# Three 64-row score products for two heads at once, q and k split whole, and a new order of the mixer

## The chip, the core and the metric

The kernel runs on one core of a Trainium2 chip. The metric is the device time of one execution in microseconds, the median of the runs. The engines are TensorE (PE in the profile, its weight loads PEld), VectorE (DVE), ScalarE (ACT), GpSimd (POOL) and SyncE (SP), which issues most transfers.

## The reference, cut to what matters

One layer of an encoder over 512 positions of width 1024: a half-step gated feed-forward, a mixer, a second half-step feed-forward, and a final norm. The mixer's attention part is what the change touches most:

```python
h = rms_norm(x, mix_norm)
u = h @ w_in                      # fourier group (512) | q (8x64) | k (2x64) | v (2x64)
q = rms_norm(q.reshape(b, s, N_Q_HEADS, HEAD_DIM), q_norm)
k = rms_norm(k.reshape(b, s, N_KV_HEADS, HEAD_DIM), k_norm)
q, k = apply_axial_rope(q, tables), apply_axial_rope(k, tables)
...
scores = jnp.einsum('bqhgd,bkhd->bhgqk', q_blk, k).astype(jnp.float32) * scale
p = jax.nn.softmax(scores, axis=-1).astype(v.dtype)
return jnp.einsum('bhgqk,bkhd->bqhgd', p, v)
```

Everything is float32. Eight query heads of 64 channels share two key heads (heads 0 to 3 the first, 4 to 7 the second). The mixer's other half is a two-dimensional Fourier transform with a small linear map for each of four channel groups, and both halves go through one output projection.

## The kernel before

**Two-part products.** TensorE multiplies in a rounded form of float32 (`F32R`). To keep float32's accuracy each operand is split into a high part (a rounded copy, made by ACT with `nc.scalar.copy`) and a low part (what is left, made by DVE in `lows`), and a product is made as three: high by high, high by low, low by high (`product`). Most of the kernel is such products over 128 rows of contraction and 512 positions.

**Stages.** `ffn` runs the first feed-forward: an opening of four gate and up chunks (`opening1`), then chunks made with fewer products (`seven`), and `down`. Its channel sums of squares are turned into a row that scales the outcome: `norm.column` or `sums` sums them on PE, `power` takes the root on POOL, and `row` turns the result on PE (L263) and copies it on ACT. Before the change `opening1` calls `row()` inside the last of its eight steps, after four of that step's twelve products. `tail` (chunk `2 * NF`, the half chunk that is left of 2752 channels) follows the opening.

**The mixer** is written as named steps (`op("name")`), each a few instructions of one engine, and the string `ORDER` names all of them in the order in which every engine's instructions are put in its queue. The engines run their queues in order. Names used below: `k.0` to `k.7`, `q0.0` ... are the eight steps (three products each) of a projection; `wk.r`, `wk.h`, `wk.l` load, round and subtract its weights; `n1.c` turns the running sums of squares `acc` on PE, and DVE then reduces them; `k.sq` squares k, `k.pq` turns the squares on PE, `k.s0` reduces them on DVE, `k.s1` takes the root on POOL, `kw` spreads it on DVE, `kp` turns it on PE and `km` multiplies k by it; `s` is a score step, `m` its maximum on DVE, `e` the exponential on ACT, `g` the reciprocal of the sum, `n` the scaling on ACT, `t` the turn of the probabilities on PE, `h` and `l` their split, `v` the product with the values.

**Scores.** A tile of q holds two heads, one of each key head, in rows 0 to 63 and 64 to 127. Before the change each head has a tile of its own, `qa` or `qb`, with the high part of its 64 channels in one half of the rows and the low part in the other, and the keys lie twice in `kst`, as high over low and as low over high. So two products over all 128 rows give the sum of all four part products of one head, one query block and all 512 keys:

```python
nc.tensor.matmul(turned(sps[n]), q, turned(kst[b][0]), start=True, stop=False)
nc.tensor.matmul(turned(sps[n]), q, turned(kst[b][1]), start=False, stop=True)
```

There are 4 tiles of q, 2 heads and 4 query blocks, so 32 score steps of two products (L1207, L1208).

**Banks.** The eight PSUM banks are handed out by `bank_for` and come back when `read` has been called for each reader.

Of the kernel before, what the change touches and what calls it, by code (L numbers as in the profile page):

```python
# [10 lines left out]
ALU = mybir.AluOpType  # L11
# [38 lines left out]
wk.r wq2.r wq0.r wq1.r wk.h wk.l wv.r k.0 k.1 wq0.h k.2 wq0.l k.3 wq1.h k.4 k.5 k.6 k.7 n1.c k.sq q0.0 cos  # L50
wq2.h q0.1 k.pq q0.2 q0.3 n1.m k.rc f0.r q0.4 q0.5 k.s0 q0.6 wq2.l k.s1 q0.7 k.sw q0.sq q2.0 wq1.l kw kp wv.h
q0.pq q1.0 k.rs q0.rc q2.1 q1.1 q1.2 q0.s0 q1.3 km q1.4 q0.sw k0.0 wv.l k1.0 q1.5 q1.6 q0.rs q0.ah q0.bh k0.3
q1.7 k0.2 k1.1 q1.sq k1.3 k0.1 q2.2 wq3.r q2.3 q1.sw q0.al q0.s1 k1.2 v.0 q0.bl q2.4 s001 s002 q1.rc s011
wq3.h m001 s010 m011 pos q2.5 s013 v.1 q1.sd q2.6 m010 e011 q2.7 e001 m002 m013 wq3.l s012 e002 s000 e010
e013 v.2 m012 f1.r q2.sq q2.sw v.3 q1.rs f0.h q3.0 v.4 e012 s003 g01 g02 v.5 f3.r m003 q1.ah q1.pq q3.1 v.6
q2.sd m000 q3.2 n002 v.7 q1.bh n001 q1.s0 n012 q1.al e000 e003 q1.s1 q1.bl f1.h s103 n1.p q3.3 g00 q3.4 g03
q2.rc vt n000 q3.5 n003 vp m103 t000 f1.l vs t003 n011 f0.l n010 q3.6 e103 n013 q3.7 t001 h000 h001 t002
q2.rs q3.sw s101 l001 v.h f00.0 l000 f2.r h002 m101 s110 q2.bh s111 l002 v.l f02.0 m111 q2.bl q3.sq f2.h o0.r
f00.1 s100 e101 f00.u m110 m100 e111 t011 g11 q3.sd s112 v000 v001 m112 h003 q2.pq h011 f02.1 l003 l011 v002
s113 s102 q2.ah q2.s0 n101 q2.s1 e100 e110 v003 t010 n111 f02.e h010 m113 t012 q2.al m102 h012 e113 e102  # L60
q3.rc o00.c t013 g13 f03.0 e112 l010 f02.h g10 f2.l f03.1 f01.0 fw.r o1.r n103 n100 v010 s213 l012 q3.pq g12
h013 o00.a q3.rs n102 f01.1 m213 f3.h f01.u q3.s0 v011 s203 v012 l013 t100 e213 fw.h m203 n110 t101 h100 h101
t102 f3.l t103 v013 l100 f10.0 o01.c q3.ah f10.1 f03.e s210 l101 h102 o01.a f03.h e203 s202 n112 l102 g23
q3.bh s212 v100 m210 n113 n203 v101 m212 h103 e210 fw.l q3.s1 m202 f12.0 t113 f02.l f12.1 r0.h l103 f10.u
q3.al s201 t110 v102 s200 v103 o4.r e212 h113 r0.l f12.e f03.l t111 t112 n213 e202 m200 f11.0 h110 o10.c l110
o10.a f13.0 m201 o2.r h111 e200 f12.h e201 g20 s211 q3.bl o0.h g22 o3.r l111 n200 m211 s303 f11.1 e211 m303
f13.1 n202 map1 f11.u v110 o1.h o5.r l113 map0 o0.l h112 f13.e f12.l d00 s313 map0.h v111 g21 l112 e303
map0.l n201 m313 map1.h s301 d01 f13.h d0.h t200 n210 d10 m301 f13.l d11 h200 n212 d1.h v112 t201 d0.l v113
map1.l c0.s l200 h201 o6.r d1.l t203 o11.c l201 t202 c0.c c0.q c1.s o11.a h203 e313 e301 h202 s312 v200 l203
c0.o c1.c m312 v201 n211 l202 s310 s311 c1.q e312 t210 g33 c0.h t213 h210 o2.h d20 d21 d2.h v202 t211 c1.o  # L70
v203 m310 e310 l210 t212 h211 c1.h d30 m311 h212 o2.l s300 n303 d2.l l211 e311 v210 l212 d31 c2.c c0.l h213
v211 m300 l213 d3.h n313 s302 m302 g31 c2.s v212 e300 c1.l v213 y0.0 y2.0 e302 g30 c2.q o21.c d3.l g32 n311
y2.1 n310 n312 c3.s o1.l c2.o c2.h n302 n300 y0.1 y1.0 c3.c o21.a t311 c3.q o7.r o20.c n301 y1.1 t310 c2.l
y0.2 y2.2 h310 y1.2 c3.o t300 c3.h o20.a t302 t301 l310 h300 c3.l l300 h302 v310 y0.3 r1.h l302 h301 h311
l301 v300 y2.3 t312 l311 v301 t303 v311 h303 t313 h312 r1.l l303 l312 v302 h313 y0.4 v303 y0.5 v312 l313 v313
r2.h y1.3 o30.c y1.4 o31.c y2.4 o30.a o31.a r2.l y1.5 y0.6 r3.h r3.l y0.7 y2.5 o5.h y0.x y0.q y1.6 y1.7 y2.6
o5.l y2.7 y1.x y2.x y5.0 o3.h y5.1 o3.l o6.h y5.2 y2.q o6.l y5.3 y5.4 y3.0 y1.h y3.1 y5.5 y3.2 y2.h y1.l y3.3
y1.q y6.0 y5.6 y5.7 y6.1 y3.4 o4.h o4.l y5.x y3.5 y6.2 y3.6 y3.7 y1.a y0.h y4.0 y0.l y3.x y4.1 y6.3 y3.h y5.h
y4.2 y4.3 y2.l y6.4 o7.h y4.4 o7.l y6.5 y4.5 y4.6 y2.a y4.7 y6.6 y7.0 y3.q y6.7 y7.1 y7.2 y3.a y5.q y7.3 y4.x
y4.q y7.4 y3.l y4.a y5.a y5.l y6.x y7.5 y6.q y6.a y7.6 y6.h y7.7 y6.l y4.h y7.x y4.l y7.q y7.a y7.h y7.l  # L80
# [8 lines left out]
def encoder(ctx, tc, A, out):  # L89
# [89 lines left out]
    def turned(ap):  # L179
        return ap.rearrange("p (a b c) -> p b a c", b=4, c=4)  # L180
# [103 lines left out]
    def ffn(norm, after, wgu, wd, wdt, groups, opening, closing):  # L284
# [6 lines left out]
        with tc.tile_pool(name=f"act{n_}", bufs=1) as ap, tc.tile_pool(name=f"sums{n_}", bufs=2) as sp:  # L291
# [288 lines left out]
            for gi, group in enumerate(groups):  # L580
# [4 lines left out]
                else:  # L585
# [6 lines left out]
                    pss["t"] = [gate(2 * NF)]  # L592
# [128 lines left out]
    def opening1(gate, column, row):  # L721
# [39 lines left out]
        def products(k):  # L761
            hi, lo = ws[k // 2]
            passes = [(c, w, m) for w, m in ((hi, hh), (hi, hl), (lo, hh)) for c in range(4)]
            for n, (c, w, m) in enumerate(passes):
                if (k, n) == (6, 8):
                    sums()
                if (k, n) == (7, 4):
                    row()
                nc.tensor.matmul(
                    turned(pss[c]), w[:, k % 2, c], turned(m[k]), start=False, stop=k == KD - 1 and w is lo,  # L770
                    skip_group_check=True,
                )
# [39 lines left out]
    with tc.tile_pool(name="mix", bufs=1) as mp, tc.tile_pool(name="mixt", bufs=1) as mt:  # L812

        room(mp, 96)
        kst = [[mp.tile([P, S], F32R, name=f"ks{v}{o}") for o in range(2)] for v in range(2)]
# [153 lines left out]
        def query_ops(t):  # L969
# [3 lines left out]
            @op(f"{name}.ah")  # L973
# [627 lines left out]
```

## Time and profile before

| what | value |
|---|---|
| median of 3 runs | 818.72 us |
| lowest run | 818.27 us |
| profiled execution | 818.38 us |
| its span, first to last instruction | 816.6 us |
| PE busy | 809.8 us, 99% |
| DVE busy | 652.4 us, 80% |
| ACT busy | 503.2 us, 62% |
| granted TensorE clock, mean | 0.998 |

A profile row names the line, the engine, the operation, and what it writes and reads; then the count, and the busy time with the mean duration of one in ns, or, in the order of time, the start and the length in us. What stands in brackets is how long the engine had been idle before it and what ended that. "mix" is any of the mixer's banks, "ring" the ring of weight slots, "near" the tiles of q, of the values and of the Fourier half, "ks" the keys.

### The profile page before, as it was taken

The numbers are of one execution on the slowest core, as the hardware profiler recorded it, in microseconds if no ns is written. First come the engines' busy times: TensorE is split into PE (matmuls) and PEld (weight loads), VectorE is DVE, ScalarE is ACT, GpSimd is POOL, SyncE is SP. The second block draws the span as 40 slices with busy tenths as digits, with TensorE's granted clock in tenths as the row PEclk, the third lists the DMA queues.
The fourth block names the chain that finished last, engine by engine and source line by source line (L and its number), as shares of the span: only waits on it lengthen the run. The fifth ranks groups of instructions, "written<-read, shape, count | busy, mean of one in ns | idle before, by whom it ended". The sixth has DMA issues, their size and how long they took to land.

```text
span 816.6 us, 13031 instructions
## 1 busy us (share of the span) xinstructions
PE 809.8 (99%) x4943; PEld 729.3 (89%) x4943; DVE 652.4 (80%) x1083; ACT 503.2 (62%) x871; POOL 67.7 (8%) x75
## 2 busy tenths in 40 slices
PE   9999999999999999999999999999999999999997
PEld 7888998899989998889998888889988998899987
DVE  7997997489856857799998578999955997489674
ACT  7873774267624735699998449557733674267462
POOL 0320000000000000221000003100100000000001
PEclk9999999999999999999999999999999999999999
DMA  7874553345443423442201236554543553345222
GB/s 258 198 172 172 146 132 89 125 130 168 85 151 89 126 67 117 130 149 65 65 26 53 78 109 140 128 188 143 133 116 110 154 145 81 132 130 143 62 78 103
DMA packets 37823, 99.75 MB, mean 122 GB/s; under 512 B 4481, under 2 KB 11265, under 8 KB 37761
## 3 DMA queue, kind: packets, MB, share of 16 engines
q1 hardware_dynamic: 28064, 82.87, 31.2%
q0 software_dynamic: 8832, 15.34, 11.1%
q8 instruction: 38, 0.62, 0.3%
q10 hardware_dynamic: 864, 0.72, 0.3%
q14 instruction: 25, 0.20, 0.1%
HBM read 93.41 MB, written 2.10 MB: 117 GB/s over the span
## 4 chain that ended last, share of the span: by engine, by line
PE 94%; DMA 2%; ACT 1%; DVE 1%; issue 1%; POOL 0%; SPq 0%; POOLq 0%; DVEq 0%; ACTq 0%
PE dn L186 26%; PE r L436 11%; PE mix L186 8%; PE gu L186 8%; PE r L441 8%; PE q L436 4%; PE r L432 4%; PE q L441 4%; PE p L432 4%; PE q L432 4%; PE p L441 2%; PE mix L1267 2%; PE mix L1233 2%; PE mix L1071 1%; PE mix L1072 1%; PE mix L1073 1%
## 5 line engine op out<-in xcount | busy, mean ns | idle before, releaser
L186 PE MATMUL dn<-at,ring 128*128 128x512 f32 x900 | 202.7, 380 | 0.0
L186 PEld LDWEIGHTS dn<-at,ring 128*128 128x128 f32 x900 | 168.0, 188 | 28.9 <-DVE ring L130 0.3
L441 PE MATMUL r<-rt,ring 128*128 128x256 f32 x560 | 154.3, 276 | 0.0
L436 PE MATMUL r<-rt,ring 128*128 128x256 f32 x840 | 147.0, 276 | 0.0
L436 PEld LDWEIGHTS r<-rt,ring 128*128 128x128 f32 x840 | 127.0, 188 | 1.6
L441 PEld LDWEIGHTS r<-rt,ring 128*128 128x128 f32 x560 | 105.1, 188 | 0.2
L391 ACT CAST ring<-s 128x1024 fp32r<-128x1024 f32 x70 | 73.6, 1051 | 35.4 <-PE r L436 16.4
L130 DVE TENSOR_TENSOR ring<-s,ring 128x1024 fp32r<-128x1024 f32 x70 | 85.1, 1216 | 12.6 <-ACT ring L391 10.3
L575 DVE SCALAR_TENSOR_TENSOR gx<-dn,gx 128x512 f32<-128x512 f32 x61 | 41.8, 688 | 63.0 <-PE dn L186 63.0
L172 ACT CAST ring<-raw_dn 128x768 fp32r<-128x768 f32 (+3 forms) x58 | 45.3, 784 | 71.3 <-PE dn L186 55.2
L441 PE MATMUL q<-rt,ring 128*128 128x256 f32 x280 | 77.0, 275 | 0.0
L160 POOL DMA_DIRECT2D ring<-in_wgu x38 | 32.9, 866 | 470.1 <-ACT u L450 372.0
L130 DVE TENSOR_TENSOR ring<-raw_dn,ring 128x768 fp32r<-128x768 f32 (+3 forms) x58 | 51.5, 890 | 9.9 <-ACT ring L172 5.9
L441 PEld LDWEIGHTS q<-rt,ring 128*128 128x128 f32 x280 | 52.6, 188 | 0.0
L130 DVE TENSOR_TENSOR ring<-raw_g,ring 128x1024 fp32r<-128x1024 f32 x35 | 42.6, 1218 | 10.1 <-PE p L432 9.5
L436 PE MATMUL q<-rt,ring 128*128 128x256 f32 x280 | 49.8, 277 | 0.0
L432 PE MATMUL r<-rt,ring 128*128 128x512 f32 x140 | 48.7, 384 | 0.2 <-ACT u L489 0.2
L186 PE MATMUL gu<-ring 128*128 128x512 f32 x216 | 48.9, 381 | 0.0
L432 PE MATMUL q<-rt,ring 128*128 128x512 f32 x140 | 48.3, 382 | 0.0
L432 PE MATMUL p<-rt,ring 128*128 128x512 f32 x140 | 48.3, 382 | 0.0
L186 PEld LDWEIGHTS gu<-ring 128*128 128x128 f32 x216 | 40.4, 188 | 6.9
L391 ACT CAST ring<-raw_g 128x1024 fp32r<-128x1024 f32 x35 | 36.8, 1051 | 15.0 <-DMA raw_g<-in_wgu 12.0
(282 smaller groups left out, 1659.3 us busy)
## 6 DMA issues: line engine op xcount, KB each, us to landing
raw_g<-in_wgu SPq DMA_DIRECT2D x35, 512.0 KB, 3.7
raw_u<-in_wgu SPq DMA_DIRECT2D x35, 512.0 KB, 4.4
raw_dn<-in_wd SPq DMA_DIRECT2D x40, 384.0 KB, 3.2
ring<-in_wgu POOLq DMA_DIRECT2D x35, 256.0 KB, 4.3
raw_gu<-in_wgu SPq DMA_DIRECT2D x12, 512.0 KB, 3.6
raw_o<-in_wo SPq DMA_DIRECT2D x8, 512.0 KB, 3.5
raw_dn<-in_wd SPq DMA_DIRECT2D x8, 448.0 KB, 3.4
raw_wq<-in_wins SPq DMA_DIRECT2D x4, 512.0 KB, 3.6
```

What stands on the lines that cost most here:

```text
L130: nc.vector.tensor_tensor(out=lo, in0=src, in1=asf(hi), op=ALU.subtract)
L160: nc.gpsimd.dma_start(out=lo, in_=src, accum_op=ALU.add)
L172: nc.scalar.copy(hi[:, :n, :], raw[:, :n, :])
L186: nc.tensor.matmul(ps, a, b, start=first and b is mhi and a is whi, stop=last and a is wlo)
L391: nc.scalar.copy(hi, src)
L432: nc.tensor.matmul(turned(ps), whi[:, ks], turned(m), start=start, stop=False, skip_group_check=True)
L436: nc.tensor.matmul(ps[:, t], whi[:, ks], m[:, o * HALF :][:, t], start=start and o == 0, stop=False, skip_group_check=True,)
L441: nc.tensor.matmul(o, wlo[:, ks], m, start=False, stop=stop, skip_group_check=True)
L575: nc.vector.scalar_tensor_tensor(out=x[d][:, t], in0=ps[:, t], scalar=0.5, in1=x[d][:, t], op0=ALU.mult, op1=ALU.add)
L1071: nc.tensor.matmul(ps, hh[k][:, cs], whi[:, a, :], start=k == 0, stop=False)
L1233: nc.tensor.transpose(pts[n][:, c * P : (c + 1) * P], prob[t, b, c][:, kc * P : (kc + 1) * P], ident)
L1267: nc.tensor.matmul(turned(outs[t, b]), w, turned(p), start=kc == 0 and i == 0, stop=kc == 3 and i == 1)
```

## The change

Four things are changed.

1. A score step works on both heads of a tile of q. `qa` now holds the high part and `qb` the low part of the whole tile, `kst[0]` and `kst[1]` those of the keys. For each of the three part products there is one product over rows 0 to 63 (first head) and one over rows 64 to 127 (second head), into two banks; the two alternate. 16 steps of six products take the place of 32 steps of two.
2. Rounding and subtracting q and k is one instruction each over 128 rows, in place of four over 64 rows for each tile of q and eight for k.
3. The maxima of both heads go to one tile of two columns, with one small product for both.
4. The row of the first norm is turned in the tail's chunk, after the first of its eight steps, and no longer in the opening; and `ORDER` is a new one.

```diff
@@ ffn, first group
-                    pss["t"] = [gate(2 * NF)]
+                    pss["t"] = [gate(2 * NF, {} if row else {1: lambda: row.append(norm.row())})]
@@ opening1, products
-                if (k, n) == (7, 4):
-                    row()
@@ query_ops and key_ops
-            @op(f"{name}.ah")
-                nc.scalar.copy(qa[t][0:HD], rots[name][0:HD])
-            @op(f"{name}.al")
-                lows(qa[t][HD:P], rots[name][0:HD], qa[t][0:HD])
-            @op(f"{name}.bh")
-                nc.scalar.copy(qb[t][HD:P], rots[name][HD:P])
-            @op(f"{name}.bl")
-                lows(qb[t][0:HD], rots[name][HD:P], qb[t][HD:P])
+            @op(f"{name}.h")
+                nc.scalar.copy(qa[t], rots[name])
+            @op(f"{name}.l")
+                lows(qb[t], rots[name], qa[t])
...
+            op("k.h")(lambda: nc.scalar.copy(kst[0], rots["k"]))
+            op("k.l")(lambda: lows(kst[1], rots["k"], kst[0]))
@@ score_ops
-                q = (qa, qb)[b][t][:, c * P : (c + 1) * P]
-                sps[n] = bank_for(f"s{n}")
-                nc.tensor.matmul(turned(sps[n]), q, turned(kst[b][0]), start=True, stop=False)
-                nc.tensor.matmul(turned(sps[n]), q, turned(kst[b][1]), start=False, stop=True)
+                sps[n] = [bank_for(f"s{t}{b}{c}") for b in range(2)]
+                cs = slice(c * P, (c + 1) * P)
+                for i, (w, m) in enumerate(((qa[t], kst[0]), (qa[t], kst[1]), (qb[t], kst[0]))):
+                    for b in range(2):
+                        r = slice(b * HD, (b + 1) * HD)
+                        nc.tensor.matmul(
+                            turned(sps[n][b]), w[r, cs], turned(m[r]), start=i == 0, stop=i == 2,
+                            skip_group_check=True,
+                        )
...
-                mxs[n] = mx = tp.tile([P, 1], F32, tag="mx", bufs=8, name=f"mx{n}")
-                nc.vector.tensor_reduce(out=mx, in_=sps[n], axis=AX.X, op=ALU.max, negate=True)
+                mxs[n] = mx = tp.tile([P, 2], F32, tag="mx", bufs=8, name=f"mx{n}")
+                for b in range(2):
+                    nc.vector.tensor_reduce(out=mx[:, b : b + 1], in_=sps[n][b], axis=AX.X, op=ALU.max, negate=True)
                 nc.vector.tensor_tensor(out=mx, in0=mx, in1=f, op=ALU.mult)
@@ ORDER, the start
-wk.r wq2.r wq0.r wq1.r wk.h wk.l wv.r k.0 k.1 wq0.h k.2 wq0.l k.3 wq1.h k.4 k.5 k.6 k.7 n1.c k.sq q0.0 cos
+wq1.r wq0.r wk.r wk.h wk.l wq0.h k.0 cos f1.r k.1 k.2 k.3 k.4 k.5 n1.c wq1.h k.6 wq1.l wq0.l k.7 q0.0 wq2.r q0.1 k.sq
```

What the order of the instructions becomes at three places follows. Lines of the changed program are some numbers lower (L1207 and L1208 are L1190 there, `product` is L182, `lows` L126).

On PE, the first score steps. Before, one head at a time (`ks00` and `ks01` are the two key tiles of the first head, `ks10` and `ks11` of the second):

```order
L186 MATMUL mix4_3304<-ring_61 128x4x32x4 x3
L1207 MATMUL mix3_3303<-ks00_3287,near_3293 128x4x32x4
L1208 MATMUL mix3_3303<-ks01_3288,near_3293 128x4x32x4
L1207 MATMUL mix0_3300<-ks00_3287,near_3293 128x4x32x4
L1208 MATMUL mix0_3300<-ks01_3288,near_3293 128x4x32x4
L1207 MATMUL mix6_3306<-ks10_3289,near_3293 128x4x32x4
L1208 MATMUL mix6_3306<-ks11_3290,near_3293 128x4x32x4
```

Now (`ks0` holds the high, `ks1` the low parts of both heads):

```order
L182 MATMUL mix4_3302<-ring_61,more_3293 128x4x32x4 x6
L1190 MATMUL mix1_3299<-ks0_3287,near_3291 128x4x32x4
L1190 MATMUL mix0_3298<-ks0_3287,near_3291 128x4x32x4
L1190 MATMUL mix1_3299<-ks1_3288,near_3291 128x4x32x4
L1190 MATMUL mix0_3298<-ks1_3288,near_3291 128x4x32x4
L1190 MATMUL mix1_3299<-ks0_3287,near_3291 128x4x32x4
L1190 MATMUL mix0_3298<-ks0_3287,near_3291 128x4x32x4
```

The two heads now alternate between two banks, and a step has six products. Steps that follow each other make blocks: in the whole mixer the 96 products stand in eight blocks, 18, 6 and six times 12.

On DVE, where the first feed-forward ends and the mixer begins (`gx` holds x; `ring` and `more` hold weights and the norm's output; `acc1` the sums of squares). Before:

```order
L575 SCALAR_TENSOR_TENSOR gx_69<-dn0_7_3_3244,gx_69 128x512
L130 TENSOR_TENSOR ring_61<-raw_wq0_3315,ring_61 128x1024
L216 SCALAR_TENSOR_TENSOR ring_61<-gx_69,ring_61 128x512
L228 TENSOR_TENSOR acc1_103<-acc1_103,sq1_7_0_3270 128x512
L1354 TENSOR_REDUCE ms1_105<-mix1_3301 128x4
```

Now:

```order
L571 SCALAR_TENSOR_TENSOR gx_69<-dn0_7_3_3244,gx_69 128x512
L126 TENSOR_TENSOR more_3293<-raw_wq1_3309,more_3293 128x1024
L126 TENSOR_TENSOR ring_61<-raw_wq0_3311,ring_61 128x1024
L212 SCALAR_TENSOR_TENSOR ring_61<-gx_69,ring_61 128x512
L224 TENSOR_TENSOR acc1_103<-acc1_103,sq1_7_0_3270 128x512
L1344 TENSOR_REDUCE ms1_105<-mix1_3299 128x4
```

The subtraction of `wq1` now stands ahead of the norm's last step and of the last addition into `acc1`. On ACT the cast of `wq1` moves in the same way, to just behind that of `wq0` and ahead of the norm's last step.

On PE at the same place, the projections of k (`mix0`) and q0 (`mix2`) and the turns of `acc1` (`n1.c`), of the squares of k (`k.pq`) and of `kw` (`kp`). Before:

```order
L186 MATMUL dn0_7_3_3244<-at0_129,ring_61 128x4x32x4 x18
L186 MATMUL mix0_3300<-ring_61 128x4x32x4 x24
L1350 MATMUL mix1_3301<-ident_107,acc1_103 128x128 x4
L186 MATMUL mix2_3302<-ring_61 128x4x32x4 x6
L954 MATMUL mix3_3303<-ident_107,sq_k_3354 128x128 x4
L186 MATMUL mix2_3302<-ring_61 128x4x32x4 x18
L186 MATMUL mix4_3304<-ring_61 128x4x32x4 x3
L1007 MATMUL mix5_3305<-ident_107,kw_3308 128x128 x4
```

Now:

```order
L182 MATMUL dn0_7_3_3244<-at0_129,ring_61 128x4x32x4 x18
L182 MATMUL mix0_3298<-ring_61 128x4x32x4 x18
L1340 MATMUL mix1_3299<-ident_107,acc1_103 128x128 x4
L182 MATMUL mix0_3298<-ring_61 128x4x32x4 x6
L182 MATMUL mix2_3300<-ring_61 128x4x32x4 x12
L948 MATMUL mix3_3301<-ident_107,sq_k_3361 128x128 x4
L182 MATMUL mix2_3300<-ring_61 128x4x32x4 x9
L182 MATMUL mix4_3302<-ring_61,more_3293 128x4x32x4 x3
L182 MATMUL mix5_3303<-ring_61 128x4x32x4 x3
L182 MATMUL mix2_3300<-ring_61 128x4x32x4 x3
L993 MATMUL mix6_3304<-ident_107,kw_3306 128x128 x4
```

`n1.c` stands six products of k earlier, `k.pq` two steps of q0 later, and `kp` follows it after 18 products in place of 21.

More of the change, by code (lines that the diff above doesn't have):

```diff
@@ L49 @@
 ORDER = """
-wk.r wq2.r wq0.r wq1.r wk.h wk.l wv.r k.0 k.1 wq0.h k.2 wq0.l k.3 wq1.h k.4 k.5 k.6 k.7 n1.c k.sq q0.0 cos
[L51 to L54, printed above, removed]
@@ L1217, in _ @@
[L1217 to L1224 removed]
+            for b in range(2):
+                @op(f"e{t}{b}{c}")
+                def _(b=b):
+                    if t not in zs:
+                        zs[t] = tp.tile([P, 4, 2], F32, tag="z", bufs=2, name=f"z{t}")
+                    prob[t, b, c] = temp(f"e{t}{b}{c}")
+                    nc.scalar.activation(
+                        prob[t, b, c], sps[n][b], AF.Exp, bias=mxs[n][:, b : b + 1], scale=f[:, b : b + 1],
+                        accum_out=zs[t][:, c, b : b + 1],
+                    )
+                    read(f"s{t}{b}{c}")
@@ L1331, in encoder @@
             position_ops(t)
+            for c in range(4):
+                score_ops(t, c)
             for b in range(2):
```

80 lines of the change are left out of this document (30 added, 50 removed).

## The prediction

> **What bounds the kernel now.** I read the page first (busy shares, clock, chain), then busy time by stage, then the order of time at four places.
>
> ```profile
> PE 809.8 (99%) x4943; PEld 729.3 (89%) x4943; DVE 652.4 (80%) x1083; ACT 503.2 (62%) x871; POOL 67.7 (8%) x75
> PEclk9999999999999999999999999999999999999999
> PE 94%; DMA 2%; ACT 1%; DVE 1%; issue 1%; POOL 0%; SPq 0%; POOLq 0%; DVEq 0%; ACTq 0%
> ...
> 330.10:352.00 21.90, 21.90 (x108) 18.50 (x107) 18.14 (x28) 16.77 (x25) 5.79 (x5) 1.00 0.55 180
> 352.00:434.00 82.00, 81.95 (x544) 74.39 (x543) 78.50 (x166) 78.06 (x156) 6.94 (x4) 1.00 0.21 65
> ```
>
> TensorE (PE) is the bound: 99% busy, at full clock, and 94% of the chain that ended last. The two stage rows (length, then busy time of PE, PEld, DVE, ACT, POOL) are the start of the mixer and the attention stage. DVE and ACT are 95% busy in the second, yet PE idles 0.05 us in 82.00. So work taken from DVE and ACT gains nothing; a PE product more or less, or a new PE wait, moves the end by its full size. A product over 512 columns is listed with 0.38 us but the next one starts earlier, so I price products by their starts:
>
> ```profile
> 352.23 0.38 PE L1208 MATMUL mix<-ks,near 128*128 128x512 f32 x1
> 352.45 0.39 PE L1207 MATMUL mix<-ks,near 128*128 128x512 f32 x1
> 352.67 0.38 PE L1208 MATMUL mix<-ks,near 128*128 128x512 f32 x1
> ...
> 371.58 0.28 PE L1072 MATMUL mix<-ring 128*128 128x256 f32 x1
> 371.70 0.28 PE L1073 MATMUL mix<-ring 128*128 128x256 f32 x1
> 371.81 0.28 PE L1071 MATMUL mix<-ring 128*128 128x256 f32 x1
> ...
> L1207 PE MATMUL mix<-ks,near 128*128 128x512 f32 x32 | 12.6, 394 | 0.1
> L1208 PE MATMUL mix<-ks,near 128*128 128x512 f32 x32 | 12.3, 384 | 0.0
> L1208 PEld LDWEIGHTS mix<-ks,near 128*128 128x128 f32 x32 | 6.0, 188 | 0.8
> ```
>
> A score product costs 0.22 us of PE (352.23, 352.45, 352.67). A product over 256 columns costs about 0.115 us although each loads its own weights, so a weight load needs no more than that when it runs beside other work. There are 32 + 32 score products: 64 x 0.22 = 14.1 us.
>
> **The base** is the profiled execution, 818.38 us with a span of 816.6; the median of the runs, 818.72, is 0.04% above it.
>
> **Term 1, the score products.** 64 products over 128 rows become 96 over 64 rows, in 48 pairs: one product of a pair uses rows 0 to 63 and the other rows 64 to 127, they share neither rows nor a bank, and they stand next to each other. No row of the trace has a product over 64 rows, so I bound it. If both of a pair run side by side, the nearest rows are the 512-column product (0.22 us) and two weight loads at the pace of the 256-column rows (2 x 0.115 = 0.23): 48 x 0.23 = 11.0. If they run one after the other, 96 x 0.22 = 21.1. I take the first, since nothing that one product holds is needed by the other: -3.0 us, with -3.5 (0.22 a pair) and +7.0 as ends. The Trainium skill (TensorEngine Tiling (Array Packing), Key Properties) states that different tiles can load and multiply in parallel; no run here shows it yet.
>
> **Term 2, changing between 128 and 64 rows.** The 16 score steps stand in 8 blocks, so there are 16 changes. One may cost nothing, or the tail of a product that the next one otherwise covers: 0.38 - 0.22 = 0.16 us. I take the middle, 0.08: +1.3 us (0 to 2.6). The Trainium skill (the same page, Key Properties) says that changing the tiling mode drains TensorE; by that rule each change would pay the tail, and the sum would be 819.7. No row here has such a change.
>
> **Term 3, the row of the first norm moves.**
>
> ```profile
> 22.88 2.04 PE L769 MATMUL gu<-ring,at 128*128 128x512 f32 x8
> 23.94 1.53 POOL L258 TENSOR_TENSOR r<-ms,mhalf 128x4 f32<-128x4 f32 x1 [22.63 <-DVE ms L251]
> 25.52 0.65 PE L263 MATMUL rp<-ident,r 128*128 128x128 f32 x4 [0.60 <-POOL r L258]
> ```
>
> Here PE waits for a power on POOL. The eight products end at 24.92, so the next could have started at 24.92 - 0.16 = 24.76; it starts at 25.52. After the change eight more opening products and three of the tail's stand ahead of the turn, 11 x 0.22 = 2.4 us, which hides the wait: -0.8 us (at least the 0.60 shown). What reads the row then comes about 1.6 us later, in a stage where PE has two whole gate chunks ahead (2 x 24 x 0.22 = 10.6 us) before a bank must come free.
>
> **Term 4, the sums of squares are turned two steps earlier (`n1.c`), and what they need is ready later.**
>
> ```profile
> 330.09 1.05 ACT L877 CAST ring<-raw_wq 128x1024 fp32r<-128x1024 f32 x1 [1.77 <-PE dn L186]
> 330.12 5.44 PE L186 MATMUL mix<-ring 128*128 128x512 f32 x24
> 330.31 0.69 DVE L575 SCALAR_TENSOR_TENSOR gx<-dn,gx 128x512 f32<-128x512 f32 x1 [0.61 <-PE dn L186]
> 331.05 0.71 ACT L212 ACTIVATE ring<-gx 128x512 fp32r<-128x512 f32 x1
> 331.17 1.23 DVE L130 TENSOR_TENSOR ring<-raw_wq,ring 128x1024 fp32r<-128x1024 f32 x1 [0.17 <-ACT ring L877]
> 332.31 0.75 DVE L216 SCALAR_TENSOR_TENSOR ring<-gx,ring 128x512 fp32r<-128x512 f32 x1
> 332.98 0.68 DVE L228 TENSOR_TENSOR acc<-acc,sq 128x512 f32<-128x512 f32 x1
> 335.39 0.60 PE L1350 MATMUL mix<-ident,acc 128*128 128x128 f32 x4
> ```
>
> Before, the last addition into `acc` ends at 333.66 and PE turns it at 335.39, after 24 products of k: no wait. Now the turn stands after 18 of them, so PE is there at 330.12 + 18 x 0.22 = 334.1. But ACT rounds `wq1` ahead of the last norm step, and DVE subtracts `wq1` and `wq0` ahead of it: ACT starts `wq0` at 330.09 and `wq1` at 331.05, which ends at 332.1; DVE, in order, starts one subtraction there and the next 1.14 later (the spacing of 331.17 and 332.31), the norm's low part 1.14 after that, at 334.4, and the addition 0.67 later, ending at 335.7. With 0.2 to 0.4 to reach PE it turns at about 336.1: +2.0 us (1.7 to 2.3). Six more products of k are queued behind it on PE and could have run; behind them wait q0 and everything else, so nothing covers it.
>
> **Term 5, the key's scale.**
>
> ```profile
> 337.16 0.60 PE L954 MATMUL mix<-ident,sq_k 128*128 128x128 f32 x4
> 337.80 0.69 DVE L959 TENSOR_REDUCE sc<-mix 128x8 f32<-128x512 f32 x1
> 338.87 2.50 POOL L965 TENSOR_TENSOR sc<-sc,mhalf 128x8 f32<-128x8 f32 x1 [52.03 <-DVE sc L961]
> 341.40 0.43 DVE L998 TENSOR_SCALAR kw<-sc 128x512 f32<-128x512 f32 x1 [0.43 <-POOL sc L965]
> 342.50 0.60 PE L1007 MATMUL mix<-ident,kw 128*128 128x128 f32 x4
> ```
>
> From `k.pq` to `kp` the chain through DVE, POOL and DVE takes 341.83 - 337.16 = 4.7 us and 0.2 or more to reach PE, 5.34 as seen. Now PE has the turn (four at about 0.11) and 6 steps of three products between the two, 0.44 + 18 x 0.22 = 4.4. I take +0.5 us (0 to 0.9).
>
> **Edits at nothing.**
>
> ```profile
> L1214 DVE TENSOR_TENSOR mx<-mx,sc 128x1 f32<-128x1 f32 x32 | 5.1, 159 | 1.4
> L130 DVE TENSOR_TENSOR near<-rot_q,near 64x512 fp32r<-64x512 f32 x8 | 5.5, 686 | 0.2
> L130 DVE TENSOR_TENSOR ks<-rot_k,ks 64x512 fp32r<-64x512 f32 x4 | 2.7, 684 | 0.0
> L976 ACT CAST near<-rot_q 64x512 fp32r<-64x512 f32 x4 | 2.5, 623 | 0.2 <-DVE rot_q L943 0.2
> ...
> 320.06 8.73 SPq L154 DMA_DIRECT2D raw_wq<-in_wins  x2
> 326.13 1.05 ACT L877 CAST ring<-raw_wk 128x1024 fp32r<-128x1024 f32 x1 [1.77 <-PE dn L186]
> raw_wk<-in_wins SPq DMA_DIRECT2D x1, 512.0 KB, 3.4
> ```
>
> Splitting q and k as a whole leaves 5 DVE subtractions of 12 and 5 ACT copies of 12, and 16 small products of maxima of 32: 7 x 0.69 + 16 x 0.159 = 7.3 us less on DVE and 7 x 0.62 = 4.3 on ACT. PE's work hides them (0.05 us idle), so 0; without that cover they would be worth at most those 0.05 us. On SP's queue `wk` moves from first to third of its weights. The third was issued at 320.06 and would land 3.4 later, at 323.5, ahead of its cast at 326.13: 0. `wq2` moves behind the cosines and `f1`; it can start when `wq1` is done at 333.3 and land near 337, and its cast stands behind the square of k, which PE releases after 337.9: 0. On POOL the tables of `pos` move behind the powers, far ahead of their first reader: 0. A score step now takes two banks at once, but the order frees them as it did.
>
> **Sum:** 818.4 - 3.0 + 1.3 - 0.8 + 2.0 + 0.5 = **818.4 us**, no change. Its own range is 815.8 (-3.5, 0, -0.8, +1.7, 0) to 820.6 (-3.0, +2.6, -0.6, +2.3, +0.9).
>
> **Rivals.** *One after the other:* the two products of a pair do not overlap. For it: every row here has full height, and starts never come closer than the columns need. Against it: disjoint rows and banks. Term 1 is +7.0 instead of -3.0: 828.4.
>
> *Half hidden weights:* a pair's loads cannot run under a product over the same rows, so a pair costs 0.115 + 0.22 = 0.335: 48 x 0.335 = 16.1, +2.0 instead of -3.0: 823.4. Against it: in the attention stage PEld is busy 74.39 us under a PE busy 81.95, so loads do run under products. The Trainium skill (TensorE: Matmul & The Clock Gate, Part 3) says weight loads overlap running products only when the row group differs; the full-height rows here speak against it, half-height ones are not in the trace.
>
> *Slower:* neither overlaps. Each of the 96 products waits for its weights and then runs alone: 96 x 0.335 = 32.2, +18.1: 839.5. It decides from 0.29 us a product (96 x 0.29 = 27.8, a total of 835.1). For it: the two halves are changed at every product. Against it: again the hidden loads.
>
> *The early turn costs nothing* (DVE is done sooner than I add up), and neither do Terms 2 and 5: 818.4 - 3.5 - 0.8 = 814.1. Against it: the order on ACT and DVE.
>
> **How the numbers follow.** Forecast 0.40; one after the other 0.20; half hidden 0.13; early turn free 0.13; neither overlaps 0.12; a gain I don't see 0.02. A change under 2% (16.4 us, so 802.3 to 835.1) is about what a measurement of this kernel can't tell from none. Only the slower rival passes it: slower 0.12, faster 0.02, same 0.86. The range, 813.5 to 829.5, takes in the free turn and the one-after-the-other case.
>
> **What would show it.** Starts of a score pair within 0.05 us and pairs 0.22 to 0.23 apart confirm Term 1; even starts 0.22 apart mean 828. A gap after each block shows Term 2. PE idle near 334 to 336, ended by DVE's `acc`, shows Term 4, and a shorter one at `kp` Term 5; none by POOL near 25 shows Term 3. I am wrong altogether if PE idles inside the attention stage for more than about 2 us, since then the new order, and not the products, sets the end.

## The result: slower by 1.3%, in two places that the forecast had priced wrongly

The changed kernel takes 829.64 us (median, 829.13 to 830.57); the kernel before took 819.12 in the same comparison. One of its four executions there lasted 1692.98 us; the ratio leaves it out, and the median of the other three is 818.72. The ratio is 1.0135, with a 95% interval of 1.0119 to 1.0151. The forecast was 818.4 and its range ended at 829.5. The profiled execution has a span of 827.5 us where it was 816.6, so 10.9 us are to be found.

The page first: busy time and instructions by engine, the granted clock in 40 slices, and the chain that ended last by engine.

```profile
PE 814.1 (98%) x4975; PEld 727.5 (88%) x4975; DVE 646.2 (78%) x1060; ACT 498.8 (60%) x864; POOL 68.2 (8%) x75
PEclk9999999999999999999999999999999999999999
PE 89%; DMA 3%; DVE 3%; ACT 2%; issue 1%; POOL 1%; SPq 0%; DVEq 0%; POOLq 0%; ACTq 0%
```

DVE has 6.2 us less work and ACT 4.4 less, about as worked out (7.3 and 4.3), and the time did not fall. TensorE's busy time grew by 4.3 us, and its share of the chain fell from 94% to 89%: other engines now hold it up. The view of waits names them for TensorE (who waits, for whom, total us, times, longest):

```profile
PE dn L182 <- DVE at L126: 2.3, 2, 2.0
PE mix L993 <- DVE kw L984: 2.2, 1, 2.2
PE mix L1340 <- DVE acc L224: 1.6, 1, 1.6
PE dn L182 <- ACT at L168: 1.0, 1, 1.0
```

Two are at the mixer's start (L1340 is `n1.c`, L993 is `kp`), and two are where the forecast saw nothing: at the down products of the *first feed-forward* (`dn`). Marks on TensorE divide the loss. The mixer's first product starts at 335.09 and not at 330.12, 5.0 us later; from there to the first product of the second feed-forward it takes 159.99 and not 153.97, 6.0 more; the rest, to the start of TensorE's last product, takes 326.93, before 327.03.

**The first feed-forward.** In the order of time on ACT and DVE, after and then before:

```profile
28.45 1.05 ACT L168 CAST at<-raw_gu 128x1024 fp32r<-128x1024 f32 x1 [2.96 <-DMA raw_gu<-in_wgu]
29.53 1.06 ACT L155 ACTIVATE at<-at 128x1024 fp32r<-128x1024 f32 x1
30.50 0.57 ACT L267 COPY rb<-rp 128x512 f32<-128x512 f32 x1
31.09 0.69 DVE L655 TENSOR_TENSOR g0p<-gu,rb 128x512 f32<-128x512 f32 x1 [4.35 <-ACT rb L267]
```

```profile
26.21 0.59 ACT L271 COPY rb<-rp 128x512 f32<-128x512 f32 x1 [1.42 <-PE rp L263]
26.83 2.72 DVE L349 SCALAR_TENSOR_TENSOR b<-gx,rp 128x512 f32<-128x512 f32 x4 [0.79 <-ACT rb L271]
```

The row is needed on DVE, through a copy that ACT makes (`rb`). Before, that copy started at 26.21. Now the turn on TensorE comes a little later in the program, and in ACT's queue the copy has come to stand behind a cast of weights (28.45) that waits 2.96 us for its transfer, and a second pass over them. It starts at 30.50. DVE stands still for 4.35 us and resumes at 31.09, 4.26 later than before. DVE's queue has changed too: before, the four instructions for `b` came first and `g0p` after them, at 29.47; now `g0p` comes first, and `b` starts at 32.30. Can DVE make the delay up? Windows of eight microseconds (length, then busy time of PE, PEld, DVE, ACT, POOL, then the granted clock), before and then after:

```profile
30.00:38.00 8.00, 8.00 (x38) 6.84 (x37) 8.00 (x18) 7.97 (x16) 4.98 (x5) 1.00 0.90 168
38.00:46.00 8.00, 8.00 (x38) 6.84 (x37) 8.00 (x16) 7.10 (x16) 4.55 (x5) 1.00 0.86 157
46.00:54.00 8.00, 8.00 (x38) 6.80 (x38) 7.88 (x16) 6.78 (x13) 0.60 (x1) 1.00 1.00 227
54.00:62.00 8.00, 8.00 (x38) 6.84 (x37) 7.64 (x12) 5.86 (x9) 0.92 (x1) 1.00 0.58 140
62.00:70.00 8.00, 8.00 (x38) 6.83 (x37) 6.57 (x12) 2.17 (x4) 0.00 (x0) 1.00 0.66 226
```

```profile
54.00:62.00 8.00, 7.40 (x33) 5.62 (x31) 7.74 (x15) 5.06 (x9) 0.00 (x0) 1.00 0.51 180
62.00:70.00 8.00, 5.28 (x15) 3.99 (x16) 7.93 (x14) 3.82 (x8) 0.92 (x1) 0.79 0.62 150
```

It cannot. DVE was full from 30 to 46 already, idled 0.48 us from 46 to 62 and had its first real room only after that. From 22 to 62 us it now idles 5.8 us in all where it idled 1.8. The delay is carried along until the down products want what DVE makes, and TensorE waits there:

```profile
56.20 0.71 PE L182 MATMUL dn<-at 128*128 128x512 f32 x2 [0.39 <-DVE at L126]
62.75 0.71 PE L182 MATMUL dn<-at 128*128 128x512 f32 x2 [0.97 <-ACT at L168]
65.43 0.80 PE L182 MATMUL dn<-at 128*128 128x512 f32 x1 [1.96 <-DVE at L126]
66.03 0.63 PE L529 MATMUL dn<-at,wt 128*128 128x512 f32 x1
66.45 0.63 PE L530 MATMUL dn<-at,wt 128*128 128x512 f32 x1
66.88 2.41 PE L182 MATMUL dn<-at 128*128 128x512 f32 x6
```

The waits add up to 3.3 us. Behind the last of them the products start 0.42 to 0.43 apart (66.03, 66.45, 66.88) and not 0.22, and the granted clock of that window is 0.79 where it was 1.00: the trace has the clock at half from 65.33 to 68.75, from near the end of the last wait on. The Trainium skill (TensorE: Matmul & The Clock Gate, Part 1) states 426.7 ns from start to start for 512 columns at the low clock; the trace agrees.

**The mixer's start.** On TensorE, ACT, DVE and POOL, in the order of time:

```profile
340.87 0.63 PE L1340 MATMUL mix<-ident,acc 128*128 128x128 f32 x4 [1.63 <-DVE acc L224]
343.35 1.04 ACT L871 CAST ring<-raw_wq 128x1024 fp32r<-128x1024 f32 x1
344.41 2.76 ACT L913 ACTIVATE sw_k<-mix,qkg 32x512 f32<-32x512 f32 x4
345.31 0.60 PE L948 MATMUL mix<-ident,sq_k 128*128 128x128 f32 x4
347.20 0.75 DVE L930 SCALAR_TENSOR_TENSOR rot_k<-mix,qkg,cos 128x512 f32<-128x512 f32 x1 [4.57 <-ACT sw_k L913]
347.87 1.22 DVE L126 TENSOR_TENSOR ring<-raw_wq,ring 128x1024 fp32r<-128x1024 f32 x1
349.00 0.69 DVE L953 TENSOR_REDUCE sc<-mix 128x8 f32<-128x512 f32 x1
350.06 1.96 POOL L959 TENSOR_TENSOR sc<-sc,mhalf 128x8 f32<-128x8 f32 x1 [58.25 <-DVE sc L955]
352.06 0.43 DVE L984 TENSOR_SCALAR kw<-sc 128x512 f32<-128x512 f32 x1 [0.85 <-POOL sc L959]
352.54 1.11 PE L993 MATMUL mix<-ident,kw 128*128 128x128 f32 x4 [2.22 <-DVE kw L984]
```

The turn of the sums waits 1.63 us for `acc`, as Term 4 said. At `kp` TensorE waits 2.22. The squares of k are turned by 345.9, but DVE reduces them only at 349.00: in its queue stand first the rotation of k (347.20, `k.rc`), which itself stood 4.57 us waiting for ACT's four pieces of `sw_k` (`k.sw`; the rotation does not read `sw_k`, but both read the bank of k), and then a subtraction of weights (`wq2.l`). The new order names `k.sw` ahead of `k.rc` and both ahead of `k.s0`. The four turns of `kp` then take 1.11 us, where `k.pq`, which is as large, took 0.60: the clock is at half again, from 352.05 to 355.47.

**The scores.** TensorE and its weight loads round one block of twelve products (two score steps), then all 96 grouped by form (min, median and max ns):

```profile
388.46 0.38 PE L1256 MATMUL mix<-pl,near 128*128 128x512 f32 x1
388.78 1.61 PE L1190 MATMUL mix<-ks,near 64*128 64x512 f32 x12
390.31 0.50 PE L1256 MATMUL mix<-ph,near 128*128 128x512 f32 x1
390.65 0.40 PE L1256 MATMUL mix<-pl,near 128*128 128x512 f32 x1
...
388.77 1.20 PEld L1190 LDWEIGHTS mix<-ks,near 64*128 64x128 f32 x12 [0.34 <-issue]
390.31 0.19 PEld L1256 LDWEIGHTS mix<-ph,near 128*128 128x128 f32 x1 [0.34 <-issue]
...
L1190 PE MATMUL mix<-ks,near x96: 374/386/494, 361.6 to 438.3; 64*128 64x512 f32 x96
```

Twelve products last 1.61 us from the first start to the last end; one after another they would last 11 x 0.22 + 0.38 = 2.80. The records start in twos: at 388.776 and 388.779, at 389.106 and 389.110, at 389.334 and 389.337. So the two products of a pair run at once and pairs are 0.22 apart, but the first pair of a block takes 0.33. At either end the weight loads stand still for 0.34 us, and the full product ahead (388.46) and the one behind (390.31) occupy 0.31 and 0.34 and not 0.22 each. Counted over the whole block and both edges (from the start of the product ahead to the second start behind, less 0.22 for each of those two), the twelve cost 1.75 us, and 1.76 in the mean of the six such blocks, where six pairs at 0.22 are 1.32: a block costs 0.44 us beyond its pairs. All eight blocks so counted take 14.62 us; the 64 products before take 14.85 by the same count.

### The profile page after: what moved, and what is told of

Its sections match the earlier page's. It is cut to its first block, busy times and chain, and to the rows that moved or that the text cites. A ratio compares the mean times of both kernels' runs of the same rounds, so it can differ in the third digit from the quotient of the medians.

```text
span 827.5 us, 13060 instructions
## 1 busy us (share of the span) xinstructions
PE 814.1 (98%) x4975; PEld 727.5 (88%) x4975; DVE 646.2 (78%) x1060; ACT 498.8 (60%) x864; POOL 68.2 (8%) x75
## 4 chain that ended last, share of the span: by engine, by line
PE 89%; DMA 3%; DVE 3%; ACT 2%; issue 1%; POOL 1%; SPq 0%; DVEq 0%; POOLq 0%; ACTq 0%
PE dn L182 25%; PE r L432 12%; PE mix L182 8%; PE r L437 8%; PE gu L182 4%; PE q L432 4%; PE q L437 4%; PE r L428 4%; PE p L428 4%; PE q L428 4%; PE p L437 2%; PE mix L1256 2%; PE mix L1222 2%; PE mix L1190 2%; PE mix L1052 1%
## 5 line engine op out<-in xcount | busy, mean ns | idle before, releaser
L182 PE MATMUL dn<-at,ring 128*128 128x512 f32 x900 | 202.8, 380 | 0.0
L182 PEld LDWEIGHTS dn<-at,ring 128*128 128x128 f32 x900 | 168.0, 188 | 28.9 <-DVE ring L126 0.3
L126 DVE TENSOR_TENSOR ring<-s,ring 128x1024 fp32r<-128x1024 f32 x70 | 85.3, 1218 | 12.6 <-ACT ring L387 10.6
L126 DVE TENSOR_TENSOR ring<-raw_dn,ring 128x768 fp32r<-128x768 f32 (+3 forms) x58 | 51.5, 891 | 8.8 <-ACT ring L168 4.4
L126 DVE TENSOR_TENSOR ring<-raw_g,ring 128x1024 fp32r<-128x1024 f32 x35 | 42.7, 1220 | 10.1 <-PE p L428 9.5
L182 PE MATMUL gu<-ring 128*128 128x512 f32 x216 | 49.2, 382 | 0.0
L182 PEld LDWEIGHTS gu<-ring 128*128 128x128 f32 x216 | 40.3, 188 | 6.9
```

The costliest lines, as they stand in the source:

```text
L126: nc.vector.tensor_tensor(out=lo, in0=src, in1=asf(hi), op=ALU.subtract)
L182: nc.tensor.matmul(ps, a, b, start=first and b is mhi and a is whi, stop=last and a is wlo)
```

## Experiments

Each is the changed kernel with an edit, if nothing else is said. "Mended" names the kernel of the third experiment. Stage lengths are read off the profiled executions:

| kernel | median us | mixer starts | mixer lasts | scores with edges |
|---|---|---|---|---|
| before | 818.72 | 330.12 | 153.97 | 14.85 |
| changed | 829.64 | 335.09 | 159.99 | 14.62 |
| row put back | 824.97 | 330.23 | 158.60 | 14.56 |
| order mended | 824.52 | 336.93 | 154.86 | 14.61 |
| both | 820.36 | 330.90 | 155.17 | 14.60 |
| heads apart | 830.36 | 335.20 | 160.28 | 14.53 |
| full height, mended | 823.02 | 330.77 | 158.33 | 17.48 |
| row later, mended | 821.30 | 330.29 | 154.96 | 14.78 |
| row copied by DVE | 824.79 | 329.46 | 160.25 | 14.62 |
| more blocks, mended | 822.20 | 333.31 | 156.96 | 16.84 |
| mended, row in the tail by DVE | 819.92 | 329.67 | 154.91 | 14.72 |
| before, row in the tail by DVE | 818.50 | 330.26 | 153.97 | 14.83 |
| mended further | 819.78 | 329.53 | 155.07 | 14.64 |

The kernel before took 819.15 in the comparison of the first four, 819.27 in that of the next four, and 819.03 in that of the last three. What follows the mixer takes 326.8 to 327.1 in some profiled executions and about 328 in others, with 0.8 us of it in two waits for DVE in the second feed-forward; no edit goes with the longer one, so stages are compared and not spans alone.

**The row put back** into the opening.

```diff
-                    pss["t"] = [gate(2 * NF, {} if row else {1: lambda: row.append(norm.row())})]
+                    pss["t"] = [gate(2 * NF)]
@@ opening1, products
+                if (k, n) == (7, 4):
+                    row()
```

> The changed kernel with one part undone: the first norm's row is turned in the opening again, as before the change; scores, splits and order stay. Theory A (the late row keeps DVE idle for 4.35 us near 27 to 31 us, and DVE, which is full in that stretch, hands this on to PE in the first group's down products, with a slower clock after PE's idle time): the mixer starts 5.0 us earlier, at 330.1 in place of 335.1 us, total 824.6. Rival B (what PE loses near 55 to 68 us has another cause, the row only moved PE's own 0.8 us wait): 830.4.

It took 824.97 us, a ratio of 1.0072 (1.0057 to 1.0087). The mixer starts at 330.23, as before the change. The move of the row cost some 4.7 us, and Theory A holds. In the profiled execution TensorE still waits 1.63 us for `acc` and 2.25 at `kp`, but the granted clock stays at 1.00 and the four turns of `kp` take 0.66 us: the mixer is 1.4 us shorter than in the changed kernel, with waits as long.

**The order mended**, three moves in `ORDER`.

```diff
-... k.5 n1.c wq1.h k.6 wq1.l wq0.l k.7 q0.0 ...
-... k.pq wq2.h q0.4 q0.5 k.sw q0.6 k.rc q1.0 wq2.l k.s0 ...
+... k.5 wq1.h k.6 wq1.l wq0.l k.7 n1.c q0.0 ...
+... k.pq k.rc wq2.h q0.4 q0.5 k.sw q0.6 q1.0 k.s0 wq2.l ...
```

> The changed kernel with three moves at the start of the new order alone: n1.c after k.7 again, k.rc ahead of k.sw, and wq2.l behind k.s0. Theory A (PE's two idle times there, 1.6 us at n1.c and 2.2 us at kp, come from where these steps stand on PE and DVE, and 1.2 us more from a slower clock after the second): about 4.5 us less, 825.1. Rival B (the chain through q0 to the first score is the limit, so the wait only moves there): 828 to 830.

It took 824.52 us, 1.0070 (1.0055 to 1.0085). The mixer shrank by 5.1 us, to 154.86; the row's loss is still there. Theory A holds.

**Both mends.**

> Both of the above together, the new scores and splits stay. Theory A: the losses add, 829.6 - 5.0 - 4.5 = 820.1, within 1.5 us of the kernel before. Rival B (the new score products themselves cost the time, whatever stands around them): 825 or more.

It took 820.36 us, 1.0018 (1.0008 to 1.0027): the two losses are separate and together make up 9.3 us of the 10.5. TensorE's waits that are left:

```profile
PE rp L259 <- POOL r L254: 0.9, 1, 0.9
PE busy L698 <- PEq L1576: 0.8, 1, 0.8
PE mix L995 <- DVE kw L986: 0.2, 1, 0.2
```

The first is the wait that the kernel before had too, the second stands ahead of the first product, and of the third only 0.2 is left.

**Heads apart.** Within a score step the three products of the first head, then the three of the second.

```diff
-                for i, (w, m) in enumerate(((qa[t], kst[0]), (qa[t], kst[1]), (qb[t], kst[0]))):
-                    for b in range(2):
+                for b in range(2):
+                    for i, (w, m) in enumerate(((qa[t], kst[0]), (qa[t], kst[1]), (qb[t], kst[0]))):
```

> The changed kernel with the six products of a score step in another order: the three of the first head, then the three of the second. Theory A (two products run at the same time only where neighbours in the queue use different rows, so a step takes 4 to 5 times 0.22 us in place of 3): 16 steps at 0.88 to 1.10 us, 14.1 to 17.6 us against 13.0 now, total 830.7 to 834.2. Rival B (PE finds the pair whatever the order in the queue): 829.6, no difference.

It took 830.36 us, 1.0134 (1.0117 to 1.0151), with the scores at 14.53: no loss. Theory A falls. The same block of twelve in the order of time:

```profile
389.10 1.61 PE L1190 MATMUL mix<-ks,near 64*128 64x512 f32 x12
```

It lasts 1.61 us again, and its records start at 389.104 and 389.114, then 389.434 and 389.445. In the queue the first three products all use the same rows. Were they started strictly in the queue's order, the second head's first product could start only with the third of the first head's, 0.44 us in, and the twelve, worked out from 0.22 a product, would need 0.66 us more. In the trace the two records that raise a semaphore, as the last product of each head does, are those of the third pair (389.665 and 389.666). So products over one half of the rows get ahead of earlier ones over the other half.

**Full height.** The mended kernel with the 128-row scores of before, and with the separate splits of q and k that these need, in the new order.

```diff
-                nc.scalar.copy(qa[t], rots[name])
...
+                nc.scalar.copy(qa[t][0:HD], rots[name][0:HD])
+                nc.scalar.copy(qb[t][HD:P], rots[name][HD:P])
...
-                    for b in range(2):
-                        r = slice(b * HD, (b + 1) * HD)
...
+                for b in range(2):
+                    for i in range(2):
...
+                            turned(sps[n][b]), (qa, qb)[b][t][:, cs], turned(kst[b][i]), start=i == 0, stop=i == 1,
```

> The mended kernel (row in the opening, start of the order mended) with the score step as before the change: two products over 128 rows for each head, q and k split in halves again; one step still takes both heads. Theory A (pairs run 0.22 us apart, 48 x 0.22 = 10.6 us, but each of 8 blocks costs 0.4 us more where the rows change, so the new scores take about 14 us, as the 64 products of before): scores 14.1 us, the total equal to the mended kernel's 820.4 within 1 us, or up to 2 us more if the longer splits of k hold up the first score. Rival B (the pairs save 3.5 us and the changes cost next to nothing): 823.4 or more, with no idle time at the first score.

It took 823.02 us, 1.0051 (1.0036 to 1.0066), 2.7 more than mended. The total is nearer to Theory B's 823.4 than to A's 820.4 to 822.4; the place is A's. A block of eight full products takes 1.76 to 1.81 us and one of twelve half-height ones 1.73 to 1.79: no difference. The loss stands in front of the first score, here and in the mended kernel:

```profile
354.39 3.20 PE L1204 MATMUL mix<-ks,near 128*128 128x512 f32 x12 [2.24 <-DVE near L126]
```

```profile
352.50 2.27 PE L1192 MATMUL mix<-ks,near 64*128 64x512 f32 x18
```

TensorE waits 2.24 us for DVE's last low part (the 17.48 us of the table hold this wait), and the granted clock stays at 1.00 behind it. In this order the split is on the path to the first score, and making it whole is worth 2.2 to 2.7 us there; A had allowed for up to 2.

**The row later**, but still in the opening: in the mended kernel, at the ninth product of the last step and not the fifth.

```diff
-                if (k, n) == (7, 4):
+                if (k, n) == (7, 8):
```

> The mended kernel with the first norm's row four products later in the opening (behind eight of the last step's twelve). PE's wait of 0.9 us for POOL goes away, but the copy of the row on ACT now stands behind a cast that waits for a transfer until about 28.4 us. Theory A (what counts is when DVE gets the row: about 30.1 us in place of 26.8): 823 to 825. Rival B (the row may come some us later at no cost): 819.5.

It took 821.30 us, 1.0022 (1.0013 to 1.0032), 0.9 more than mended by the medians and between the two theories; the two intervals overlap, so that a loss against the mended kernel is not shown. The profiled execution, the lowest of the ten with 819.37, loses nothing: the mixer starts at 330.29, though DVE resumes late:

```profile
29.40 0.69 DVE L655 TENSOR_TENSOR g0p<-gu,rb 128x512 f32<-128x512 f32 x1 [2.77 <-ACT rb L267]
```

That is 2.6 us later than before. So a delay of 2.6 can pass without harm, and one of 4.3 cost 5. Whether the other executions, 820.0 to 821.9, lost something here no profile shows; the number of A is refuted, the number of B not reached.

**The row copied by DVE.** The row stays in the tail; its copy is made by DVE for the first norm. (The expectation speaks of several norms; the edit changes this one alone.)

```diff
-            nc.scalar.copy(self.rb[:, t], ps[:, t])
+            (nc.scalar.copy if self.n else nc.vector.tensor_copy)(self.rb[:, t], ps[:, t])
```

> The changed kernel as it is, with the row's copy moved from ACT to DVE, for all norms but the closing ones that have n above 0. Theory A (ACT's queue, a cast that waits for a transfer and a long copy, holds the row back until 31.1 us): DVE goes on at about 28.8, 2.3 us sooner, total 827.3, with 826 to 828.5 as ends. Rival B (the place of the turn on PE alone makes it late): 829.6, or more by the 0.7 us of DVE's copy.

It took 824.79 us, 1.0068 (1.0052 to 1.0083): 4.9 less than the changed kernel, and more than A gave it. The mixer starts at 329.46.

```profile
28.32 0.69 DVE L267 COPY rb<-rp 128x512 f32<-128x512 f32 x1 [1.63 <-PE rp L259]
```

DVE makes the copy at 28.32, straight after the turn, and goes on. The turn's place on TensorE was harmless: with the turn still in the tail, the loss is gone once the copy is out of ACT's queue. B falls. The edit also brought DVE's queue back to the order of before (`b` at 28.93, `g0p` at 31.56). That order alone did not make the loss: the run before this one has the changed order (`g0p` at 29.40, `b` at 30.60), and its profiled execution loses nothing in this stage.

**More blocks.** In the mended kernel seven score steps are parted from their neighbours by other TensorE work: 15 blocks and not 8.

```diff
-s03 s01 wq3.h s00 q1.sw wv.l m03 q2.4 q2.5 v.0 ...
+s03 q2.4 s01 wq3.h q2.5 s00 q1.sw wv.l m03 v.0 ...
...
-... wq3.l v.6 e012 v.7 q1.l q3.0 q2.sw q1.s1 s12 s11 f0.h q2.sq q3.1 ...
+... wq3.l v.6 e012 v.7 q1.l q3.0 q2.sw q1.s1 s12 q3.1 s11 f0.h q2.sq ...
...
```

> The mended kernel with other PE work put between score steps that stood next to each other: 15 blocks of score products in place of 8, the same 96 products. Theory A (each block costs 0.4 us for the two changes of height): 7 x 0.4 = 2.9, total 823.3. Rival B (a change of height costs nothing by itself, the gaps come from waits for exponentials and banks): 820.4.

It took 822.20 us, 1.0036 (1.0022 to 1.0050), 1.8 more than mended. The scores with their edges went from 14.60 to 16.84, 2.24 for seven blocks or 0.32 each. A holds in kind and is somewhat large. (This profiled execution, with 825.70 the slowest of the five, reached the mixer late, which no part of the edit explains; only its scores are read.)

**Both mends, with the row in the tail and copied by DVE.** The edits of the second and the seventh experiment together.

> The changed kernel with both mends: the three orders at the mixer's start mended (the turn of the sums of squares back behind k.7, the key's rotation ahead of the square's swap, wq2's subtraction behind the key's sum), and the row of the first norm left in the tail but copied by DVE and no longer by ACT. Theory A (the two losses are separate, and the ACT queue is all that made the late row expensive): the mixer starts where it does with the copy on DVE, at 329.5, and is as long as with the mended order, 155.2; with 326.8 behind it that is a span of 811.4 from the first product, 1.4 less than with the row put back: 818.9 us, equal to the kernel before (819.2) within 0.5. Theory B (the gain at the first stage is lost again at the mixer's start, because wq's rounding on ACT sets its pace): 820.4, as with the row put back.

It took 819.92 us, 1.0012 (1.0003 to 1.0021). The mixer starts at 329.67 and lasts 154.91, both as A has them; the total is nearer to B, and the profiled execution, which is the median one, takes 328.1 us after the mixer. The stages bear A out, the median does not decide.

**The kernel before with the row in the tail, copied by DVE**: the edit to the copy, and the row moved as in the change, with nothing else of it.

> The kernel before with one thing of the change alone: the row of the first norm turned in the tail's chunk, and its copy made by DVE. Scores, splits and order are those before. Theory A: PE no longer waits for the power near 25 and nothing else moves, so the mixer starts at 329.5 in place of 330.1: 818.5 us, 0.7 less than the kernel before. Theory B (the 0.7 is made up by the wait for the weights at the mixer's start): 819.2, no difference.

It took 818.50 us, 0.9990 (0.9981 to 0.9999), against 819.03: A's total. The wait for POOL is gone from the view of waits. In the profiled execution the mixer starts no earlier all the same (330.26), since the first products, from 4.5 to 11 us and ahead of the moved row, lost 0.76; whether that is chance stays open. It is the one kernel that beats the one before, by 0.5 us, and its interval ends just short of 1.

**Mended further.** To the kernel with both mends and DVE's copy, two more moves: `n1.c` one step of q0 later, `kp` one step of q1 later.

```diff
-... k.7 n1.c q0.0 ... kw kp km q1.1 q0.sw ...
+... k.7 q0.0 n1.c ... kw q1.1 kp km q0.sw ...
```

> The kernel with both mends, and two more places of the order moved: the sums of squares are turned behind the first step of q0, and the key's scale is turned behind the second step of q1, one step of three products later each. Theory A (what the mended mixer still loses at its start, 0.25 near the turn of the sums and 0.42 at the key's scale, is wait, and a product step put ahead covers it): 0.4 to 0.7 less than with both mends alone, about 818.3 us. Theory B (the wait moves on to the next reader: the later scale delays the key's product with it, its split and the first scores): no gain, 818.9, or up to 0.5 more.

It took 819.78 us, 1.0009 (1.0000 to 1.0018), with the mixer at 155.07: nothing gained, as B has it, though its total is above B's 818.9 to 819.4. No version with the new scores came below the kernel before.

## Why the prediction was wrong

**The base** held: 819.12 in the comparison, 818.72 without the long execution, forecast 818.4.

**Term 1 (score products, -3.0)** was right in its mechanism and came out at its better end: the two of a pair start 3 ns apart (up to 29 ns), pairs 0.22 us apart, so 48 pairs take 10.6 us and 64 products took 14.1: -3.5.

**Term 2 (changes of height, +1.3) was under-sized.** By the count with edges the scores went from 14.85 to 14.62, so Terms 1 and 2 together are -0.2 and not -1.7: against the 3.5 stand 3.3 us of edges and first pairs more than before, 0.2 for each of 16 changes. About 0.5 of these are a wait inside the block of six, for ACT's exponential. A block of twelve pays 0.44, and seven added blocks paid 0.32 each, so a change costs 0.16 to 0.22. I had taken the middle of 0 and 0.16, for want of a row. The Trainium skill (TensorEngine Tiling (Array Packing), Key Properties) says that such a change drains TensorE, and by that rule I had worked out 819.7; the trace agrees with the rule and shows its price a little higher.

**Term 3 (the row moved, -0.8) failed, and cost 5.0.** The wait for POOL did go. The failed step is "What reads the row then comes about 1.6 us later, in a stage where PE has two whole gate chunks ahead". The turn itself came 1.9 us later (27.45 for 25.52), but the reader 4.3, because the copy between TensorE and DVE is on ACT, in order, behind a cast that waits for a transfer; I followed the moved instruction on its own engine and not its copy on the next. And the cover was counted on the wrong engine: TensorE had chunks ahead, but DVE had next to no idle time until 62 us and could not catch up, so its delay came out at the down products 30 us later. The row put back and the copy by DVE each take the loss away. Most of the 5.0 us are the 3.3 of waits and some 1.7 for the slower products, an estimate from 3.41 us at half the clock.

**Term 4 (`n1.c`, +2.0)** was right: TensorE idles 1.63 us for `acc`, in the place foretold, and makes the turn 1.8 us later than 18 products at 0.22 would have allowed.

**Term 5 (`kp`, +0.5) was under-sized:** 2.2 us of waiting, and some 1.4 more for the products behind it at the slow clock, by the run with the row put back, which waited as long and kept the full clock. The sum has no term for the clock, here or in Term 3. I took the chain's length from the old trace, from `k.pq` on, and let it start when TensorE had turned the squares. But `k.s0` stands in DVE's queue behind `k.rc`, which the new order puts behind ACT's `k.sw`. Mending Terms 4 and 5 together gave back 5.1 us of the mixer.

**The edits at nothing.** Less work on DVE and ACT brought nothing in the attention stage, as said. At the first score it did: with the split undone in the new order TensorE waits 2.24 us there. The moved transfers and POOL's tables caused no wait of TensorE. That the order frees the banks of a score step as it did was not quite so: in the block of six the second head's first product starts 0.52 us after the first head's, behind ACT's exponential.

**The rivals.** *One after the other* gave 828.4, close to the 829.64, and is nevertheless refuted by the starts of the pairs; *half hidden weights* and the slower rival, *neither overlaps*, fall in the same way, and *the early turn costs nothing* by the wait at `n1.c`. That a total comes out near a rival's says nothing for its mechanism. The condition for "wrong altogether" did not occur:

```profile
356.97:438.97 82.00, 81.96 (x564) 70.57 (x563) 71.57 (x139) 72.19 (x143) 10.17 (x7) 1.00 0.26 76
```

TensorE idles 0.04 us in the 82 of the attention stage. The losses lay ahead of it.

**What stays open:** the 0.9 us of mixer in the best mended versions (154.9 against 153.97), of which about 0.5 is the wait inside the block of six; the second feed-forward's two lengths; and why the clock fell behind some waits of about two microseconds and not behind others. An edit that takes away the changes of height but keeps three half-height products was not tried.

## What to carry to other kernels

When an instruction is moved, follow its result through every engine's queue to the last reader, and ask of each engine on the way whether it has idle time to catch up with; the slack of the bounding engine at that moment is not the slack of the chain. A delay on an engine that is full can surface much later, here 30 us, at an innocent line, and if the bounding engine then waits for some two microseconds, the work behind it may run slowly as well. Half-height products side by side want long blocks: here a step of six saves 0.22 us against four full products, and a block pays 0.44 for entering and leaving, so that blocks of twelve, as most are, come out even.

## What the hardware showed that I had not expected

- Products over different halves of the rows overtake each other: three and three in the queue ran as pairs about 10 ns apart (389.104 and 389.114), and the scores cost 14.53 us in that order and 14.62 in the alternating one. That every engine runs its queue in order, as said of the mixer at the start, holds for TensorE here only within one half of the rows. The Trainium skill (TensorE: Matmul & The Clock Gate, Part 3) states that products start strictly in the program's order; these starts disagree. The 4 ns between starts on different row groups that it gives there agree with the 3 ns measured.
- Weight loads for half the rows are hidden under products over the same rows: pairs come every 0.22 us although every product loads its own weights. The sentence in the same part that loads overlap only where the row group differs does not hold here.
- After a wait of 1.96 us, with others shortly before, products over 512 columns started 0.42 to 0.43 us apart until about 69 us; after one of 2.22 at `kp` four turns took 1.11 us and not 0.60. Each time the clock was at half for 3.41 us (in the run with the order mended once for 6.83). Waits of 2.25 at `kp` with the row put back and of 2.24 at the first score with full height were followed by products at the full clock, so the length of one wait does not settle it.
